# Refilling PSUM with partial sums in the opening of a two-layer decoder trunk, with eight visits instead of five

## The chip, the cores and the metric

The kernel runs on one core of a Trainium2 chip. A core has a matrix engine (TensorE, PE in the profile; its weight loads stand apart as PEld), a vector engine (VectorE, DVE), a scalar engine (ScalarE, ACT), GpSimd (POOL), and SyncE (SP), whose queue issues most transfers. TensorE accumulates in PSUM, which has eight banks of 128 x 512 float32; everything else lives in SBUF or in HBM. The metric is the device time of one execution in microseconds (us); lower is better.

## The reference

512 tokens of width 2048 go through two layers. All of it is float32.

```python
# layer 0: differential attention, 8 heads, q and k of 2 x 128, v and g of 256 a head
c_act = silu(c)
shift, scale, gate = split(c_act @ w_mod[0] + b_mod[0], 3)
h = x * (1 + scale) + shift
q, k, v, g = split(h @ a_w_in, 4)          # a_w_in: 2048 x 8192
a = softmax(q1 k1' + alibi) - lam * softmax(q2 k2' + alibi)
y = (rms_norm(a v) * (1 - lam_init) * silu(g)) @ a_w_out
x = layer_norm(alpha * x + gate * y)
# then shared keys, values and forget gates from x with its own modulation,
# and layer 1: forgetting attention with 16 heads, projections b_w_in and b_w_out
```

The part that matters here is the beginning. `h` needs `shift` and `scale`, which are products of the 2048 activated conditioning values with two 2048 x 2048 blocks of `w_mod`. `h @ a_w_in` for the first two heads can begin as soon as 128 columns of `h` (one k-tile of sixteen) are known.

## The kernel before

**Products.** Every float32 matrix is split into a high part in the matrix engine's format (`hi`, a cast on ScalarE) and the remainder (`lo`, a subtraction on VectorE). A product is three matmuls: hi x hi, hi x lo, lo x hi (`products`, lines 174 to 176).

**Weights.** `WeightStream` holds one fixed order of pieces of two k-tiles by up to 512 columns. SyncE loads a piece into one of four staging tiles (`wst`, line 47); `step` splits it into one of three pairs `whi` (line 94) and `wlo` (line 95). A pair is free again when its last product is done.

**The opening** (the block around `START`) computes `h` k-tile by k-tile and at once the first projections of heads 0 and 1. For one set of k-tiles (first k-tile 0, then 1, then pairs: `sets`) SyncE loads the modulation rows into `sms` (line 473, five buffers), VectorE multiplies them with the conditioning values and adds them up (`sacc`, lines 498 and 500; half of k-tile 1's sum is done by TensorE, line 527), TensorE adds the 128 partial rows (line 530), and VectorE adds the bias (`mcol`, line 536). Then TensorE transposes 128 columns of `x` (line 541), ScalarE writes the high part `hh` and a full copy `htmp` (lines 545 and 546), and VectorE the low part `hl` (line 550).

For each k-tile and head there are seven sums of 128 x 512: three for q and the first half of k (banks 4, 5, 6, named `sc`, `sc` and `o`) and four for v and g (banks 0 to 3, `acc`). That is 21 matmuls for a k-tile and a head. The seven sums of one head fill seven of the eight banks, and the eighth is used for sums and transposes, so only one head can be in PSUM at a time. The kernel therefore works in visits (`phases`): head 0 takes k-tiles 0 to 3, head 1 takes 0 to 7, head 0 takes 4 to 11, head 1 takes 8 to 15, head 0 takes 12 to 15. At the end of a visit `spill` brings the seven sums to SBUF: ScalarE copies them where they are the head's first (line 578), and VectorE adds them to what is there where they are not (line 580).

**Order.** VectorE's order in the opening is the order of the program, which the string `START` spells: a digit is that many multiply-adds of modulation rows, `c` finishes a set and starts its column sums, `m` adds the bias, `t` turns a k-tile, `l` writes its low part, `s` splits the next weight piece, `g` does the products of the next k-tile of a visit. The order of the other engines' instructions is fixed by a planner when the kernel is built: it takes, among instructions that are ready by its own estimate, the one earliest in the program. Each engine then runs its own list strictly in that order; SyncE's transfers too.

After the opening, heads 0 and 1 use the sums in `part`, and the third and later heads are projected in groups that keep all sixteen k-tiles in PSUM.

Of the kernel before, what the change touches and what calls it, by code (L numbers as in the profile page):

```python
# [11 lines left out]
F32R = mybir.dt.float32r  # L12
I32 = mybir.dt.int32
AF = mybir.ActivationFunctionType
ALU = mybir.AluOpType

P = 128
# [10 lines left out]
ET = mybir.EngineType  # L28


START = "cmtlssg6c6t1lgcst4g3tsl9sggts8sl6s2gtggts7lgsstlgg2s7gstl2ss9gsgtslgg5stgg6lsstg2gss8sggt2g4l4sgstctslggtslssggssgggg"
LAM_INIT = 0.8 - 0.6 * math.exp(-0.0)


# [76 lines left out]
def tile_yoco(  # L111
# [24 lines left out]
    V, S, PE, G = nc.vector, nc.scalar, nc.tensor, nc.gpsimd  # L136
# [7 lines left out]
    hpool = ctx.enter_context(tc.tile_pool(name="hpool", bufs=32))  # L144
# [20 lines left out]
    def o_bank(name="o"):  # L165
        return ps.tile([P, 512], F32, name=name, tag="o", bufs=1)
# [2 lines left out]
        S.copy(hi, src)  # L169
        V.tensor_tensor(lo, src, hi.bitcast(F32), op=ALU.subtract)  # L170

    def products(dst, lhs, rhs, start, stop):

        PE.matmul(dst, lhs[0], rhs[0], start=start, stop=False)  # L174
        PE.matmul(dst, lhs[0], rhs[1], start=False, stop=False)  # L175
        PE.matmul(dst, lhs[1], rhs[0], start=False, stop=stop)  # L176


    ident = const.tile([P, P], F32, name="ident")
# [79 lines left out]
    ws = WeightStream(nc, wpool)  # L259
# [38 lines left out]
    Hh = [None] * KT  # L298
    Hl = [None] * KT
# [5 lines left out]
    def group(job, natural, evac, banks=range(4), bg=0, before_sub=None, after_sub=None, hold=0, after_held=None):  # L305
# [7 lines left out]
        def burst(s, b, hi, lo):  # L313
            nonlocal count
            for kk in range(2):
                kt = 2 * s + kk
                bs = slice(b * P, (b + 1) * P)
                start, stop = kt == 0, kt == KT - 1
                if natural:
                    products(acc[b][:, :w], (Hh[kt][:, bs], Hl[kt][:, bs]), (hi[kk][:, :w], lo[kk][:, :w]), start, stop)  # L320
                else:
                    products(acc[b], (hi[kk][:, bs], lo[kk][:, bs]), (Hh[kt], Hl[kt]), start, stop)
            if s == ns - 1:
                evac(b, acc[b])
            tick(bg(count) if callable(bg) else bg)
            count += 1
# [113 lines left out]
    part = {}  # L440
    with tc.tile_pool(name="start", bufs=2, reuse_waits="tile") as sp, tc.manual_schedule(engines={ET.DVE}):
# [18 lines left out]
        loaded = {}  # L460
# [91 lines left out]
        acc = {}  # L552
        wsub = {}

        def first_products(u, kt, start, stop):
            s, kq = kt // 2, kt % 2
            if start:
                acc[u] = [acc_bank() for _ in range(4)] + [sc_bank(), sc_bank(), o_bank()]
            for m, job in enumerate(first[u]):
                if kq == 0:  # L560
                    wsub[u, m] = ws.get(job, s, 0)
                hi, lo = wsub[u, m]
                for b in range(3 if m == 0 else 4):
                    bs = slice(b * P, (b + 1) * P)
                    if m == 0:
                        products(acc[u][4 + b], (hi[kq][:, bs], lo[kq][:, bs]), (Hh[kt], Hl[kt]), start, stop)
                    else:
                        products(acc[u][b], (Hh[kt][:, bs], Hl[kt][:, bs]), (hi[kq], lo[kq]), start, stop)

        def spill(u):  # L570
            new = u not in part
            if new:
                part[u] = [None] * 7
            last = at["go"] == len(todo) - 1
            for b in (0, 1, 4, 6, 5, 2, 3) if last else (4, 5, 6, 0, 1, 2, 3):
                if new:
                    part[u][b] = kpool.tile([P, T], F32, name="part", tag="K")
                    S.copy(part[u][b], acc[u][b])
                else:
                    V.tensor_tensor(part[u][b], part[u][b], acc[u][b], op=ALU.add)  # L580

        todo = [(u, kt, kt == k0, kt == k1 - 1) for u, k0, k1 in phases for kt in range(k0, k1)]

# [59 lines left out]
        while at["go"] < len(todo):  # L643
            go()
            dv(4)
            split_next()
# [539 lines left out]
    acc = [acc_bank() for _ in range(TB)]  # L1186
    held = {}
    for i, (half, s) in enumerate(lag):
# [294 lines left out]
```

## Time and profile before

| | us |
|---|---|
| median of three runs | 1960.49 (1959.22 to 1961.36) |
| the profiled execution | 1958.95 |
| its span, first to last instruction | 1957.2 |
| TensorE busy | 1923.4 |
| VectorE busy | 1355.0 |
| ScalarE busy | 700.0 |
| start of the first product | 18.09 |
| start of the last product of the opening | 200.21 |

A profile is one execution. A row of instructions in order of time gives its start, its duration, the engine, the line, the operation with output and inputs, how many were merged, and in brackets how long the engine had been idle and what ended that. Rows of windows give the busy time of each engine in a stretch, the granted clock of TensorE (1.00 is full) and what the transfers did. A matmul's duration (0.39 us) is longer than the distance to the next one, because they overlap.

### The profile page before, as it was taken

The page shows a single profiled execution, that of the slowest core. Times are in us where ns is not written, and L with a number is a line of the kernel's source. Part 1 is how long each engine was busy: PE and PEld are TensorE (multiplying, and loading weights), DVE is VectorE, ACT ScalarE, POOL GpSimd, SP SyncE. Part 2 cuts the span into 40 slices and gives each one's busy share as a digit, 9 for nine tenths or more (in the row PEclk, how much of TensorE's full clock was granted, in tenths as well). Part 3 has the DMA queues.
Part 4 walks back from the last instruction along what each step waited for, and adds up shares of the span by engine and source line. Part 5 has one row for each costly group of instructions (what it writes and reads, how often), then busy time and mean ns, then how long its engine had stood idle before and what let it go on. Part 6 is the DMA issues. An engine that isn't in the chain of part 4 may idle for free.

```text
span 1957.2 us, 25652 instructions
## 1 busy us (share of the span) xinstructions
PE 1923.4 (98%) x8997; PEld 1619.0 (83%) x8997; DVE 1355.0 (69%) x2499; ACT 700.0 (36%) x1186; POOL 2.2 (0%) x10
## 2 busy tenths in 40 slices
PE   5999999999999999999999999999999999999997
PEld 4888888888888888888889998888888888888886
DVE  7886578767777778567675657776566666676657
ACT  2432444323332344531273223224343434353123
POOL 0000000000000000000000000000000000000000
PEclk8999999999999999999999999999999999999999
DMA  9983355676667675466537866775354555553622
GB/s 343 361 302 118 124 183 166 202 229 204 213 203 224 190 238 177 130 229 214 181 133 233 270 202 215 245 260 163 110 157 148 153 154 153 156 173 113 223 91 104
DMA packets 337582, 376.16 MB, mean 192 GB/s; under 512 B 67974, under 2 KB 247196, under 8 KB 336684
## 3 DMA queue, kind: packets, MB, share of 16 engines
q1 hardware_dynamic: 334496, 370.30, 58.8%
q10 hardware_dynamic: 2956, 4.22, 0.6%
q8 instruction: 71, 1.16, 0.2%
q14 instruction: 59, 0.48, 0.1%
HBM read 345.63 MB, written 28.79 MB: 191 GB/s over the span
## 4 chain that ended last, share of the span: by engine, by line
PE 93%; DVE 3%; DMA 1%; SPq 1%; issue 1%; ACT 0%; DVEq 0%; ACTq 0%
PE acc L174 28%; PE acc L175 28%; PE acc L176 28%; PE sc L174 2%; PE sc L175 2%; PE sc L176 2%; PE o L174 1%; PE o L175 1%; PE o L176 1%; DVE wlo L95 1%; SPq L473 0%; PE tr L541 0%; DMA nr<-n_dram 0%; DMA wst<-in_a_w_in_dram 0%; DVE sacc L500 0%
## 5 line engine op out<-in xcount | busy, mean ns | idle before, releaser
L94 ACT CAST whi<-wst 128x1024 fp32r<-128x1024 f32 (+3 forms) x330 | 333.5, 1011 | 736.5 <-PE acc L176 339.5
L95 DVE TENSOR_TENSOR wlo<-wst,whi 128x1024 fp32r<-128x1024 f32 (+3 forms) x330 | 385.7, 1171 | 280.6 <-ACT whi L94 267.9
L174 PE MATMUL acc<-whi,hh 128*128 128x512 f32 (+1 forms) x1296 | 494.0, 384 | 1.0 <-DVE ztmp L1007 1.0
L175 PE MATMUL acc<-wlo,hh 128*128 128x512 f32 (+1 forms) x1296 | 492.4, 380 | 0.3 <-DVE wlo L95 0.3
L176 PE MATMUL acc<-whi,hl 128*128 128x512 f32 (+1 forms) x1296 | 491.8, 380 | 0.0
L174 PE MATMUL acc<-hh,whi 128*128 128x512 f32 x1184 | 463.6, 392 | 0.0
L175 PE MATMUL acc<-hl,whi 128*128 128x512 f32 x1184 | 461.7, 390 | 0.0
L176 PE MATMUL acc<-hh,wlo 128*128 128x512 f32 x1184 | 460.9, 390 | 0.0
L174 PEld LDWEIGHTS acc<-whi,hh 128*128 128x128 f32 x1296 | 244.5, 189 | 41.0 <-DVE ztmp L1007 1.8
L176 PEld LDWEIGHTS acc<-whi,hl 128*128 128x128 f32 x1296 | 243.2, 188 | 41.7
L175 PEld LDWEIGHTS acc<-wlo,hh 128*128 128x128 f32 x1296 | 243.4, 188 | 38.9 <-DVE wlo L95 0.7
L393 DVE SCALAR_TENSOR_TENSOR macc<-ms,cact,macc 128x512 f32<-128x512 f32 x307 | 229.2, 747 | 56.3 <-DMA ms<-in_w_mod_dram 38.4
L176 PEld LDWEIGHTS acc<-hh,wlo 128*128 128x128 f32 x1184 | 222.3, 188 | 47.7
L174 PEld LDWEIGHTS acc<-hh,whi 128*128 128x128 f32 x1184 | 222.5, 188 | 43.2 <-issue 0.3
L175 PEld LDWEIGHTS acc<-hl,whi 128*128 128x128 f32 x1184 | 222.5, 188 | 42.2
L500 DVE SCALAR_TENSOR_TENSOR sacc<-sms,cact,sacc 128x512 f32<-128x512 f32 (+1 forms) x127 | 89.5, 705 | 5.7 <-DMA sms<-in_w_mod_dram 2.0
L728 ACT ACTIVATE e<-e,mn 128x128 f32<-128x128 f32 (+3 forms) x64 | 36.0, 563 | 103.0 <-DVE mn L724 102.9
L1289 ACT ACTIVATE eb<-eb,mnb 128x128 f32<-128x128 f32 (+1 forms) x64 | 36.0, 563 | 88.8 <-DVE mnb L1286 88.6
L724 DVE CUSTOM_DVE_ANT_0 e<-sc,bias 128x128 f32<-128x128 f32 (+3 forms) x64 | 31.1, 486 | 25.2 <-PE sc L176 25.2
L1286 DVE CUSTOM_DVE_ANT_0 eb<-sc,biasb 128x128 f32<-128x128 f32 (+1 forms) x64 | 31.1, 486 | 23.0 <-PE sc L176 22.4
L393 DVE SCALAR_TENSOR_TENSOR macc<-msk,cact,macc 128x512 f32<-128x512 f32 x53 | 39.7, 749 | 1.0
L1280 DVE SCALAR_TENSOR_TENSOR biasb<-nfb,F,mask 128x128 f32<-128x128 f32 (+1 forms) x64 | 34.6, 542 | 0.6
(264 smaller groups left out, 1714.9 us busy)
## 6 DMA issues: line engine op xcount, KB each, us to landing
wst<-in_a_w_in_dram SPq DMA_DIRECT2D x240, 256.0 KB, 3.8
ms<-in_w_mod_dram SPq DMA_DIRECT2D x136, 256.0 KB, 3.8
ms<-in_kv_w_mod_dram SPq DMA_DIRECT2D x64, 512.0 KB, 4.4
wst<-in_b_w_in_dram SPq DMA_DIRECT2D x128, 256.0 KB, 2.8
sms<-in_w_mod_dram SPq DMA_DIRECT2D x56, 512.0 KB, 6.8
wst<-in_kv_w_dram SPq DMA_DIRECT2D x40, 512.0 KB, 3.8
ms<-in_w_mod_dram SPq DMA_DIRECT2D x32, 512.0 KB, 4.2
wst<-in_a_w_out_dram SPq DMA_DIRECT2D x32, 512.0 KB, 4.2
```

The lines of the kernel that those rows point to most:

```text
L94: self.nc.scalar.copy(hi[:, :, :w], st[:, :, :w])
L95: self.nc.vector.tensor_tensor(lo[:, :, :w], st[:, :, :w], hi[:, :, :w].bitcast(F32), op=ALU.subtract)
L174: PE.matmul(dst, lhs[0], rhs[0], start=start, stop=False)
L175: PE.matmul(dst, lhs[0], rhs[1], start=False, stop=False)
L176: PE.matmul(dst, lhs[1], rhs[0], start=False, stop=stop)
L393: ins = V.scalar_tensor_tensor(acc, w, cact[:, kt : kt + 1], acc, op0=ALU.mult, op1=ALU.add)
L500: V.scalar_tensor_tensor(acc, w, sc, acc, op0=ALU.mult, op1=ALU.add)
L724: V.tensor_tensor_reduce(out=e[:, :w], in0=sc[:, :w], in1=st["bias"][:, (3 - i) * P :], scale=-1.0, scalar=3.0e38, op0=ALU.add, op1=ALU.mi ...
L728: S.activation(e[:, :w], e[:, :w], AF.Exp, bias=mn, scale=-1.0, accum_out=rs)
L1280: V.scalar_tensor_tensor(bias[:, :w], cur[hd, "nf"][:, :w], F[:, i, hd : hd + 1], mask[:, (3 - i) * P :], op0=ALU.add, op1=ALU.add)
L1286: V.tensor_tensor_reduce(out=e[:, :w], in0=sc[:, :w], in1=bias[:, :w], scale=-1.0, scalar=3.0e38, op0=ALU.add, op1=ALU.min, accum_out=mn)
L1289: S.activation(e[:, :w], e[:, :w], AF.Exp, bias=mn, scale=-1.0, accum_out=rs)
```

## The change

Three things change, all in the opening.

1. There are eight visits: head 0 takes k-tile 0, head 1 takes 0 and 1, head 0 takes 1 to 3, head 1 takes 2 to 5, head 0 takes 4 to 7, head 1 takes 6 to 11, head 0 takes 8 to 15, head 1 takes 12 to 15. The order of weight pieces follows the visits; a piece of two k-tiles is listed once, where it is first used.
2. A head that comes back gets its seven partial sums copied into the PSUM banks by ScalarE before its products, which then add to them (`start` is False). At the end of every visit ScalarE copies the sums out; VectorE adds nothing.
3. `START` is written anew for these visits. The first two weight pieces, which head 0 needs in two visits, are split into tiles of the pool of k-tiles, half a piece at a time, and so do not hold one of the three pairs.

```diff
-START = "cmtlssg6c6t1lgcst4g3tsl9sggts8sl6s2gtggts7lgsstlgg2s7gstl2ss9gsgtslgg5stgg6lsstg2gss8sggt2g4l4sgstctslggtslssggssgggg"
+START = "c1msstlgc8mtssg1lggcsmt2lt2lsgg4s4sgg4csmt2lt2lsgg4s4sgg4csmt2lt2lsgg4s4sgg4csmt2lt2lsgg4s44cmt2lt2lsgg4s4sggs4sggcsmt2lt2lsgg444csmtltlsggssggssgg"
...
-    def products(dst, lhs, rhs, start, stop):
+    def products(dst, lhs, rhs, start, stop, loaded=False):
...
-    phases = [(0, 0, 4), (1, 0, 8), (0, 4, 12), (1, 8, 16), (0, 12, 16)]
+    phases = [(0, 0, 1), (1, 0, 2), (0, 1, 4), (1, 2, 6), (0, 4, 8), (1, 6, 12), (0, 8, 16), (1, 12, 16)]
...
-    for u, k0, k1 in phases:
-        for s in range(k0 // 2, k1 // 2):
-            for j in first[u]:
-                ws.add(j, s)
+    for u, s in dict.fromkeys((u, k // 2) for u, k0, k1 in phases for k in range(k0, k1)):
+        for j in first[u]:
+            ws.add(j, s)
...
             if start:
                 acc[u] = [acc_bank() for _ in range(4)] + [sc_bank(), sc_bank(), o_bank()]
+                for b in (4, 5, 6, 0, 1, 2, 3) if u in part else ():
+                    S.copy(acc[u][b], part[u][b])
+            loaded = u in part
+            start = start and not loaded
...
                 if new:
                     part[u][b] = kpool.tile([P, T], F32, name="part", tag="K")
-                    S.copy(part[u][b], acc[u][b])
-                else:
-                    V.tensor_tensor(part[u][b], part[u][b], acc[u][b], op=ALU.add)
+                S.copy(part[u][b], acc[u][b])
...
-                ws.step()
+                ws.step((lambda: hpool.tile([P, 512], F32R, name="held", tag="H")) if ws.done < 2 else None)
                 ws.load(ws.done + 3)
```

More of the change, by code (lines that the diff above doesn't have):

```diff
@@ L170, in split @@
         V.tensor_tensor(lo, src, hi.bitcast(F32), op=ALU.subtract)
-    def products(dst, lhs, rhs, start, stop):
-        PE.matmul(dst, lhs[0], rhs[0], start=start, stop=False)
-        PE.matmul(dst, lhs[0], rhs[1], start=False, stop=False)
-        PE.matmul(dst, lhs[1], rhs[0], start=False, stop=stop)
+    def products(dst, lhs, rhs, start, stop, loaded=False):
+        PE.matmul(dst, lhs[0], rhs[0], start=start, stop=False, skip_group_check=loaded)
+        PE.matmul(dst, lhs[0], rhs[1], start=False, stop=False, skip_group_check=loaded)
+        PE.matmul(dst, lhs[1], rhs[0], start=False, stop=stop, skip_group_check=loaded)
     ident = const.tile([P, P], F32, name="ident")
@@ L565, in first_products @@
                     if m == 0:
-                        products(acc[u][4 + b], (hi[kq][:, bs], lo[kq][:, bs]), (Hh[kt], Hl[kt]), start, stop)
+                        products(acc[u][4 + b], (hi[kq][:, bs], lo[kq][:, bs]), (Hh[kt], Hl[kt]), start, stop, loaded)
                     else:
-                        products(acc[u][b], (Hh[kt][:, bs], Hl[kt][:, bs]), (hi[kq], lo[kq]), start, stop)
+                        products(acc[u][b], (Hh[kt][:, bs], Hl[kt][:, bs]), (hi[kq], lo[kq]), start, stop, loaded)
         def spill(u):
```

## The prediction

> **What bounds the kernel now.** I read the page's engine line and slices first, then windows over the opening, then the groups by form, last the instructions in order of time around one change of visit.
>
> The page of the kernel before (busy shares; busy tenths and granted TensorE clock in forty slices of 49 us; shares of the chain):
>
> ```profile
> PE 1923.4 (98%) x8997; PEld 1619.0 (83%) x8997; DVE 1355.0 (69%) x2499; ACT 700.0 (36%) x1186; POOL 2.2 (0%) x10
> PE   5999999999999999999999999999999999999997
> PEclk8999999999999999999999999999999999999999
> PE 93%; DVE 3%; DMA 1%; SPq 1%; issue 1%; ACT 0%; DVEq 0%; ACTq 0%
> ```
>
> TensorE is the bound, and only the first and last slices are not full. Windows: length, then busy time and instructions of PE, weight load, VectorE (DVE), ScalarE (ACT) and POOL, granted clock, DMA share, GB/s:
>
> ```profile
> 0.00:18.05 18.05, 2.64 (x10) 1.99 (x10) 8.99 (x24) 4.17 (x6) 1.61 (x9) 1.00 0.91 279
> ...
> 33.00:37.00 4.00, 3.99 (x9) 3.14 (x10) 3.23 (x5) 0.63 (x1) 0.00 (x0) 0.50 1.09 385
> ...
> 40.60:43.40 2.80, 1.68 (x12) 1.39 (x12) 2.73 (x6) 1.03 (x3) 0.00 (x0) 1.00 1.07 380
> 43.40:47.00 3.60, 3.52 (x11) 2.79 (x12) 2.43 (x4) 0.70 (x2) 0.00 (x0) 0.57 1.09 381
> 47.00:59.00 12.00, 12.00 (x54) 9.98 (x53) 11.68 (x16) 6.11 (x11) 0.00 (x0) 0.99 1.09 383
> 59.00:200.00 141.00, 141.00 (x668) 116.93 (x668) 103.70 (x146) 47.07 (x65) 0.56 (x1) 1.00 0.72 243
> 200.00:400.00 200.00, 199.83 (x952) 167.36 (x950) 146.54 (x347) 85.52 (x176) 0.00 (x0) 1.00 0.56 170
> 400.00:1957.00 1557.00, 1543.18 (x7215) 1302.73 (x7213) 1060.43 (x1933) 550.96 (x924) 0.00 (x0) 1.00 0.57 184
> ```
>
> From 59 to 200 us TensorE has no gap; VectorE is busy 104 of 141 us, so its additions there cost nothing now. After 200 nothing waits until the tail: a microsecond won or lost in the opening arrives unchanged at the end. Before 18.05 nothing changes, since the first k-tile needs the same transfers. What is left is 18.05 to 59.
>
> How much TensorE loses there: the products of L174, L175 and L176, the sums L527, then the column sums L530 and transposes L541 at full rate, and the first and last of the 21 products of one k-tile for one head:
>
> ```profile
> 18.05:59.00 40.95, 14.51 (x37) 0.87 1.09 382
> 18.05:59.00 40.95, 13.72 (x32) 0.87 1.09 382
> 18.05:59.00 40.95, 12.99 (x32) 0.87 1.09 382
> 18.05:59.00 40.95, 3.77 (x32) 0.87 1.09 382
> 59.00:200.00 141.00, 5.67 (x48) 1.00 0.72 243
> 59.00:200.00 141.00, 7.18 (x48) 1.00 0.72 243
> 195.68 0.39 PE L174 MATMUL sc<-hh,whi 128*128 128x512 f32 x1
> 200.21 0.39 PE L176 MATMUL acc<-whi,hl 128*128 128x512 f32 x1
> ```
>
> A product takes (200.21 - 195.68)/20 = 0.2265 us. In 18.05 to 59 stand 37 + 32 + 32 = 101 products, 22.9 us; the 32 sums, 3.8; twelve column sums at 5.67/48 = 0.118, 1.4; twelve transposes at 7.18/48 = 0.150, 1.8. Together 29.9 of 40.95 us: **11.0 us are lost**, in gaps and at half clock. No change of the opening can win more than that.
>
> **The change, part by part.** Durations by form (count, then busy us and mean ns; idle before):
>
> ```profile
> L94 ACT CAST whi<-wst 128x1024 fp32r<-128x1024 f32 x16 | 16.9, 1057 | 32.0 <-PE o L175 17.8 <-issue 12.2 <-ACT htmp L546 0.9
> L94 ACT CAST whi<-wst 128x512 fp32r<-128x512 f32 x2 | 1.2, 624 | 7.8 <-PE o L175 5.9 <-PE acc L176 1.8
> L545 ACT ACTIVATE hh<-tr,mcol 128x512 fp32r<-128x512 f32 x16 | 12.5, 778 | 38.9 <-PE tr L541 38.9
> L578 ACT COPY part<-acc 128x512 f32<-128x512 f32 x8 | 4.4, 613 | 0.3
> L580 DVE TENSOR_TENSOR part<-part,acc 128x512 f32<-128x512 f32 x10 | 6.3, 680 | 0.0
> L500 DVE SCALAR_TENSOR_TENSOR sacc<-sms,cact,sacc 128x512 f32<-128x512 f32 x105 | 78.9, 751 | 4.1 <-DMA sms<-in_w_mod_dram 1.2
> L95 DVE TENSOR_TENSOR wlo<-wst,whi 128x1024 fp32r<-128x1024 f32 x16 | 19.5, 1221 | 10.0 <-ACT whi L94 10.0
> L95 DVE TENSOR_TENSOR wlo<-wst,whi 128x768 fp32r<-128x768 f32 x16 | 15.2, 952 | 0.0
> ```
>
> And the visit that ends at 55 us: ScalarE's spill copies up to its next cast, and TensorE's last product into the first bank and first product of the next visit:
>
> ```profile
> 52.90 1.08 ACT L578 COPY part<-sc 128x512 f32<-128x512 f32 x2 [4.05 <-PE sc L176]
> 53.86 0.61 ACT L578 COPY part<-o 128x512 f32<-128x512 f32 x1
> 54.34 2.09 ACT L578 COPY part<-acc 128x512 f32<-128x512 f32 x4
> 56.25 1.12 ACT L94 CAST whi<-wst 128x1024 fp32r<-128x1024 f32 x1
> ```
> ```profile
> 52.47 0.39 PE L176 MATMUL sc<-hh,wlo 128*128 128x512 f32 x1
> ...
> 55.19 0.39 PE L174 MATMUL sc<-hh,whi 128*128 128x512 f32 x1
> ```
>
> *Removed:* three times seven additions on VectorE, 21 x 0.68 = 14.3 us. They lie under TensorE's full 141 us, so they win nothing by themselves.
>
> *Added on ScalarE:* five visits become eight. Spills go from 14 copies to 56, and six visits start by copying seven sums back, 42 more: 84 added. Seven spills take 56.25 - 52.90 = 3.35 us, 0.48 each. No copy into PSUM stands in the trace; the nearest rows are this 0.48 and the 0.62 of a 128x512 cast from SBUF; I take 0.5 and keep 0.48 to 0.62. That is 84 x 0.5 = 42 us more, on a ScalarE that is busy 47 of 141 us: room enough over the stage, but bunched at the changes of visit. The Trainium skill (ScalarE: Activation LUTs, Step-by-step: what each stage is for) says ScalarE writes faster to PSUM than to SBUF; by that the price is at or under 0.48, the 42 us become 40 or less, and no run here shows it yet.
>
> *A change of visit.* A bank must be finished, spilled, refilled and only then multiplied into. The old visit's last k-tile ends its banks three products (0.68 us) apart, so TensorE still has 6 x 0.68 = 4.1 us of work when the first bank is done, and uses the last bank of the new visit another 4.1 us later. ScalarE needs 14 x 0.5 = 7 us in these 8.2. If spills and refills take turns, bank n is ready 1.0(n+1) us after the first was done and is needed at 4.1 + 0.68 n: no wait (7.0 against 8.2 for the last). But a cast of 1.06 us and activations of 0.78 us for the next k-tiles want the same 8 us. Five of the six refilling visits find two k-tiles ready, so TensorE can take a ready bank twice; the visit to k-tile 1 alone cannot. Lower end 0 each; upper end as in the first rival, 2.0. I take 0.4 for five of them and 0.8 for that one: **2.8 us**.
>
> *The order of visits.* Head 1 now takes k-tiles 0 and 1 before head 0 goes on. The transfers ahead of head 1's first weights are those that stood ahead of head 0's second: the kernel before issues them at the same place in SyncE's queue and shows when they land. Rows of SyncE, ScalarE and TensorE:
>
> ```profile
> 23.54 5.01 SPq L47 DMA_DIRECT2D wst<-in_a_w_in_dram  x6
> ...
> 31.45 0.83 ACT L94 CAST whi<-wst 128x768 fp32r<-128x768 f32 x1 [12.74 <-DMA wst<-in_a_w_in_dram]
> 32.18 0.77 ACT L545 ACTIVATE hh<-tr,mcol 128x512 fp32r<-128x512 f32 x1
> ...
> 33.01 1.22 PE L174 MATMUL sc<-hh,whi 128*128 128x512 f32 x2 [1.58 <-ACT hh L545]
> ```
>
> So head 1 can start when that cast ends, at 32.3, as its k-tile 0 is long there; if k-tile 1's two activations go first, 2 x 0.7 later at 33.6. I take 32.3. From 18.05 to 32.3 TensorE does 21 products (4.8 us), the sums of k-tile 1 (3.8 + 4 x 0.118) and four transposes (0.6): 9.7 of 14.25, lost **4.6 us**. Then it is cold, as now: between 33 and 37 nine products in 4.00 us at clock 0.50 instead of 17.7, lost **2.0 us**. After that it has 63 products (14.3 us) for k-tiles 0 and 1 instead of 21, so the gap of 40.6 to 43.4 and the second cold stretch after it (clock 0.57) are covered: this is where the change can win. I estimate k-tile 2 at 48 us (VectorE does two more splits, 1.22 + 0.95, and ScalarE one train of 14 copies before it) against a need at 51; each us beyond the cover would cost one.
>
> *Later supply.* Two heads on a pair of k-tiles are 84 products, 19 us. VectorE needs for a pair 16 x 0.75 + 4 splits (2 x 1.22 + 2 x 0.95) + 2 x 0.69 = 17.7 us, so the chain stays ahead, except at k-tiles 8 to 11, which head 1 takes alone. There VectorE must do, after a split buffer comes free inside k-tile 7: a cast 1.06, a split 1.22, twelve multiply-adds 9.0 and a split 0.95, 12.2 us; then column sums 0.95, transposes 0.6, an activation 0.78, some 2.5 with the column add. TensorE has 12 products of k-tile 7 (2.7) and two k-tiles (9.5), with their transposes 13 to 14. Between 0.6 and 2.8 us open up at k-tile 10; I take **1.6 us**.
>
> *The rest.* SyncE's weight loads come earlier than modulation rows; bytes are the same, and at 383 GB/s (47 to 59 us) they bound only what is counted above. The first two splits go to eight tiles of the k-tile pool, in halves, 2.2 us on VectorE as before. Products, their count and shape stay; a product onto a refilled bank is the same instruction.
>
> *Sum.* Lost after: 4.6 + 2.0 + 1.6 + 2.8 = 11.0 us, against 11.0 now: **no change**. The profiled execution took 1958.95 us (span 1957.2), 1.5 under the median of 1960.49; I put the difference of 0.0 on the median: 1960.5 us. Least loss: without waits and gap, 6.6, that is -4.4 us. Within 0.2% means 3.9 us, about what a measurement of this kernel can tell from no change.
>
> **Rivals.**
> *Copies on the path (slower).* ScalarE's order is fixed when the kernel is built. If all seven spills stand ahead of the refills, the last spill ends 4.1 + 0.5 us after the first bank was done and the first refill at 5.1, while TensorE is free at 4.1: 1.0 us each; with a 1.06 us cast between, 2.0. Six times: 6 to 12 us instead of 2.8, +3.2 to +9.2, middle 1966.7. For it: seven copies stand unbroken at 52.90 to 56.25. Against: there was nothing to put between. It decides from 1.1 us a change on. Chance 0.28.
>
> *Short waits cool the clock (slower).* If each refilling visit starts cold, as at 33 and 43.4, six cost 2.0 more: +12, 1972.5. For it: the window of 2.80 us with 1.68 busy at 40.6 was followed by 3.6 us at 0.57. Against: waits here should be under 2 us amid dense products. The Trainium skill (TensorE: Matmul & The Clock Gate, A second HAM failure mode: psum-queue depth-cycling) describes just such micro-idling between banks that lowers the clock; but the same page (What's actually happening) lets the clock fall only after an idle window of about 3.4 us, by which waits of 2 us would cost themselves alone. Chance 0.08.
>
> *Everything is hidden (faster).* Spills and refills alternate and k-tile 10 is in time: -4.4, 1956.1; without the cold start at 32.3 another 2.0, 1954.1. For it: the sums above leave 1.2 us of room at a change. Against: five mean waits of zero. Chance 0.22.
>
> **How the numbers follow.** My forecast has 0.42, its own range -3.9 to +3.9 (a late first cast, +1.3, and the k-tile 10 bounds included): 0.36 within 0.2%, 0.02 faster, 0.04 slower. Copies on the path: 0.26 slower, 0.02 within. Clock: 0.08 slower. Hidden: 0.20 faster, 0.02 within. Faster 0.22, same 0.40, slower 0.38. The range runs from 1954.5 (nearly all of the hidden case) to 1970 (all copies on the path), leaving out the clock case and little more.
>
> **What would show it.** TensorE's first product for head 1 at 32.3 to 33.6 and no gap at 40; products dense from there; L580 gone and 84 more copies on ScalarE; idle of TensorE released by ScalarE's refill line, 0 to 1 us at each of six changes; a gap of 1 to 3 us before k-tile 10; the last product of the opening within 4 us of 200.2; nothing moved after it. I am wrong if waits on refills exceed 1.1 us each, if the clock falls after them, or if weights or k-tiles 2 and 3 come later than their cover.

## The result: 22 us slower

The changed kernel takes 1982.65 us (median of four runs, 1982.29 to 1985.63) against 1960.86 us for the kernel before beside it (1959.22 to 1961.36): a ratio of 1.0115, 95% interval 1.0102 to 1.0127. The forecast was 1960.5 us, no change; its range ended at 1970. The two profiled executions lie 26.7 us apart (1985.63 and 1958.95), 5 us more than the medians, so what the traces below count is somewhat more than the 21.8 us of the medians.

The profiled execution took 1985.63 us, the longest of the four, with a span of 1983.8. The lines of its page that answer to those of before (engines, slices of 49.6 us, granted clock, chain):

```profile
PE 1934.9 (98%) x8997; PEld 1625.3 (82%) x8997; DVE 1342.9 (68%) x2480; ACT 742.7 (37%) x1272; POOL 2.2 (0%) x10
...
PE   5988999999999999999999999999999999999997
...
PEclk9989999999999999999999999999999999999999
...
PE 92%; DVE 4%; DMA 2%; ACT 1%; issue 1%; SPq 1%; DVEq 0%; ACTq 0%
```

Two more slices are not full. Windows over the same profile (columns as in the prediction: length, busy time and instructions of PE, PEld, DVE, ACT and POOL, clock, DMA share, GB/s), and the last product of the opening:

```profile
0.00:19.25 19.25, 2.63 (x10) 1.99 (x10) 11.47 (x29) 4.35 (x8) 1.60 (x9) 1.00 0.90 275
19.25:59.00 39.75, 34.78 (x156) 28.84 (x157) 25.08 (x39) 19.98 (x34) 0.00 (x0) 0.87 0.98 329
59.00:227.00 168.00, 154.53 (x670) 124.56 (x669) 106.72 (x149) 85.54 (x143) 0.56 (x1) 0.93 0.66 218
227.00:427.00 200.00, 199.83 (x951) 167.11 (x950) 139.30 (x333) 81.94 (x166) 0.00 (x0) 1.00 0.57 170
427.00:1983.00 1556.00, 1543.13 (x7215) 1302.85 (x7214) 1060.32 (x1934) 550.91 (x924) 0.00 (x0) 1.00 0.59 185
```
```profile
226.84 0.39 PE L176 MATMUL acc<-whi,hl 128*128 128x512 f32 x1
```

The opening ends at 226.84 instead of 200.21, 26.6 us later. Behind it the two kernels are alike: 199.83 busy of 200 us, then the same 7215 TensorE instructions in 1556 and 1557 us. Where 668 TensorE instructions had filled 141 us without a gap, 670 now take 168 us with 13.5 us idle, at a mean clock of 0.93.

Counted in the traces, start in us of the n-th of the 672 products of the opening (`after` is the changed kernel; the other columns are experiments below):

| product | before | after | e4 | e11 | e17 | e18 | e19 |
|---|---|---|---|---|---|---|---|
| 84 | 55.0 | 50.4 | 50.5 | 51.0 | 45.7 | 55.2 | 46.6 |
| 126 | 65.9 | 64.9 | 60.9 | 61.4 | 57.4 | 66.2 | 56.2 |
| 168 | 76.0 | 74.6 | 72.1 | 72.6 | 67.2 | 76.1 | 69.0 |
| 252 | 96.9 | 98.8 | 93.5 | 94.1 | 89.9 | 97.1 | 91.3 |
| 336 | 117.9 | 123.1 | 116.6 | 116.1 | 114.1 | 118.0 | 113.7 |
| 420 | 138.8 | 156.7 | 143.4 | 143.7 | 147.8 | 139.2 | 137.7 |
| 504 | 159.3 | 175.8 | 163.9 | 164.8 | 167.0 | 159.7 | 158.8 |
| 588 | 180.7 | 207.7 | 193.9 | 186.0 | 198.9 | 181.5 | 179.8 |
| 672 | 200.2 | 226.8 | 213.1 | 205.2 | 218.1 | 201.0 | 199.4 |

The early gain is there: 4.6 us at product 84. Most of it is gone by product 126 and all of it by product 252; then 13 us are lost between products 336 and 420 and 10 between 504 and 588.

The first loss is at k-tile 2, whose first product is the 85th:

```profile
50.38 0.39 PE L176 MATMUL acc<-held,hl 128*128 128x512 f32 x1
...
50.60 0.95 PE L529 MATMUL tr<-ones,sacc 128*128 128x1 f32 x8
51.59 0.16 DVE L535 TENSOR_TENSOR mcol<-tr,bcol 128x4 f32<-128x4 f32 x1 [5.84 <-PE tr L529]
...
53.33 0.73 PE L174 MATMUL sc<-hh,whi 128*128 128x512 f32 x2 [0.87 <-ACT hh L544]
```

VectorE has stood still for 5.84 us when the column sums of k-tiles 2 and 3 come, behind product 84; only then can k-tile 2 be finished.

**Where it goes.** The queries of what VectorE waited for (us in total, times, longest) from 18.05 us to the end of the opening, before and then after:

```profile
DVE wlo L95 <- ACT whi L94: 17.2, 6, 5.9
DVE hl L550 <- ACT htmp L546: 13.1, 5, 3.5
DVE mcol L536 <- PE tr L530: 8.6, 6, 2.8
```
```profile
DVE mcol L535 <- PE tr L529: 28.8, 7, 8.5
DVE wlo L95 <- ACT whi L94: 23.7, 10, 5.9
DVE hl L549 <- ACT htmp L545: 14.0, 13, 2.7
```

The bias now waits 28.8 us for the column sums, 8.6 before. And TensorE's own waits from 19 to 227 us after:

```profile
PE sc L174 <- ACT hh L544: 6.9, 8, 0.9
PE tr L529 <- DVE sacc L499: 6.7, 2, 3.8
PE tr L540 <- DVE mcol L535: 5.4, 8, 3.6
```

No matmul there waits for the copies back into PSUM (line 560; by the groups, weight loads wait for them 1.8 us in all). TensorE waits for VectorE's last multiply-add, the bias and the activation: the chain that makes a k-tile. Rows in order of time, after, around k-tiles 8 to 11 (start, duration; in brackets the idle time before and what ended it):

```profile
123.06 0.39 PE L176 MATMUL acc<-whi,hl 128*128 128x512 f32 x1
...
123.28 0.95 PE L529 MATMUL tr<-ones,sacc 128*128 128x1 f32 x8
124.27 0.16 DVE L535 TENSOR_TENSOR mcol<-tr,bcol 128x4 f32<-128x4 f32 x1 [5.05 <-PE tr L529]
...
124.49 0.66 PE L540 MATMUL tr<-ident,xt 128*128 128x128 f32 x4 [0.26 <-DVE mcol L535]
125.18 0.78 ACT L544 ACTIVATE hh<-tr,mcol 128x512 fp32r<-128x512 f32 x1 [3.59 <-PE tr L540]
...
126.01 0.72 PE L174 MATMUL sc<-hh,whi 128*128 128x512 f32 x2 [0.87 <-ACT hh L544]
...
135.97 0.39 PE L176 MATMUL acc<-whi,hl 128*128 128x512 f32 x1
...
140.19 1.83 PE L529 MATMUL tr<-ones,sacc 128*128 128x1 f32 x8 [3.83 <-DVE sacc L499]
```

Until 123.06 TensorE does products without a gap, and VectorE has nothing to do for 5.05 us: its next instruction is the bias, which needs the column sums, and these stand in TensorE's list behind those products. When they are done at last, TensorE has no product left, and sums, bias, transposes and activation run one after the other with nothing beside them. Then VectorE has to do the next pair's multiply-adds, which it could have done in the 5.05 us; it isn't done when TensorE needs the sums, and TensorE stands still for 3.83 us. The two engines wait for each other in turns. Two windows of after, from one bias to the next:

```profile
75.83:100.03 24.20, 23.07 (x100) 18.60 (x100) 16.87 (x24) 13.76 (x22) 0.00 (x0) 0.93 0.93 315
100.03:124.27 24.24, 23.11 (x100) 18.68 (x100) 16.87 (x24) 13.77 (x22) 0.00 (x0) 0.93 0.78 260
```

VectorE works 16.87 us for a pair of k-tiles, and the pair takes 24.2.

**The clock.** Windows of after, ahead of and in two stretches at half clock:

```profile
98.50:101.90 3.40, 2.27 (x17) 1.84 (x16) 1.57 (x3) 0.96 (x2) 0.00 (x0) 1.00 0.70 237
101.90:105.30 3.40, 3.40 (x11) 2.71 (x12) 2.11 (x3) 1.57 (x3) 0.00 (x0) 0.50 0.10 13
136.00:139.40 3.40, 0.36 (x2) 0.00 (x0) 3.22 (x6) 0.83 (x1) 0.00 (x0) 1.00 1.08 373
139.40:149.60 10.20, 8.29 (x27) 6.71 (x28) 6.47 (x11) 2.89 (x4) 0.00 (x0) 0.50 0.75 256
```

In the opening the trace has half clock from 30.2 (6.8 us), 54.1, 78.0 and 101.9 (3.4 each), 139.4 (10.2) and 194.1 (6.8): 34 us, against 10.2 before. From product 84 to the end of the opening, intervals between TensorE's instructions add up to some 20 us of gaps and some 11 us of products and transposes slowed at half clock (each interval beyond the one at full clock, counted to at most twice that); before it was 2 to 3 and none.

### The profile page after: what moved, and what is told of

Read it like the earlier page. It is cut to its first block, busy times and chain, and to the rows that moved or that the text cites. A ratio compares the mean times of both kernels' runs of the same rounds, so it can differ in the third digit from the quotient of the medians.

```text
span 1983.8 us, 25712 instructions
## 1 busy us (share of the span) xinstructions
PE 1934.9 (98%) x8997; PEld 1625.3 (82%) x8997; DVE 1342.9 (68%) x2480; ACT 742.7 (37%) x1272; POOL 2.2 (0%) x10
## 4 chain that ended last, share of the span: by engine, by line
PE 92%; DVE 4%; DMA 2%; ACT 1%; issue 1%; SPq 1%; DVEq 0%; ACTq 0%
PE acc L174 27%; PE acc L175 27%; PE acc L176 27%; PE sc L174 2%; PE sc L175 2%; PE sc L176 2%; PE o L174 1%; DVE sacc L499 1%; PE o L175 1%; PE o L176 1%; DVE wlo L95 1%; DMA sms<-in_w_mod_dram 1%; PE tr L540 1%; DMA wst<-in_a_w_in_dram 1%; SPq L472 0%
```

## The experiments

Three accounts are set against each other. Theory A (also D, order theory or list theory): the order of VectorE's and TensorE's lists. Theory B (also refill theory): the copies back into PSUM. Theory C is in e1 to e8 that eight visits leave TensorE no products in reserve, whatever the order; in the later runs it is the transfers, or the three pairs of split weights. Edits of `START` are shown for one pair of k-tiles as it recurs; all times are medians against a kernel before of 1959.6 to 1960.3 us on the same chip. Groups of runs had different chips, so that differences between groups carry about 1 us.

**e1: sums earlier.** The column sums (`c`) stand ahead of the products of the last two k-tiles (`gg`); VectorE's list is unchanged.

```diff
-csmt2lt2lsgg4s4sgg4
+cggsmt2lt2lsgg4s4s4
```

> The changed kernel with the letters of START moved so that the column sums of a set stand in the program ahead of the last two products of the visit before; VectorE's own order stays the same instruction for instruction, as do visits, copies and products. Theory A (order of sums): the changed kernel is slow because TensorE's list has the column sums behind all products of a visit, so that VectorE waits 3.4 to 8.5 us at each bias addition and the chain of sums, bias, transposes and activation lies open at each set; then this kernel wins back most of the 26 us of the opening, 1960 to 1969 us, and VectorE's waits on the column sums fall under 2 us each. Theory B (refills): the 84 copies on ScalarE are the cost; then it stays at 1978 to 1984. Theory C (visits): eight visits leave TensorE no products in reserve, whatever the order; then it stays over 1975 too, with gaps before new k-tiles.

1979.81 us (ratio 1.0101, 1.0086 to 1.0116): only 3 us better, far from theory A's range. The wait moved on by one step, as VectorE's row for the low part shows, in the query as above, 14.0 us in the changed kernel:

```profile
DVE hl L549 <- ACT htmp L545: 36.3, 10, 9.3
```

**e4: the whole turn earlier.** Sums, bias, transposes and low parts ahead of the products that were in front of them; VectorE's list unchanged.

```diff
-csmt2lt2lsgg4s4sgg4
+csmt2lt2lggsgg4s4s4
```

> As the kernel with the sums first, but the bias, both transposes of the next two k-tiles and their low parts stand ahead of those products in the program too; VectorE's order is again the same. Theory A: the transposes now overlap with products as well, so that TensorE has no stretch of low activity between visits and no second to sixth half-clock stretch; 1957 to 1964 us, 2 to 6 us under the kernel with only the sums moved. Theory B: 1978 to 1984. Theory C: gaps at new k-tiles stay, over 1975.

1973.05 us (1.0067, 1.0052 to 1.0082): 9.6 us of the loss are TensorE's order alone, and the time lies between the ranges of the theories. Until product 336 this kernel is ahead of the kernel before; what remains is lost behind it.

**e6: only VectorE's list.** Multiply-adds of the next pair are put in front of VectorE's waits for bias and low parts.

```diff
-csmt2lt2lsgg4s4sgg4
+c5smt4lt4lsgg2s1sgg
```

> The changed kernel with its visits, copies and TensorE's order of sums behind the products; only VectorE's list is written otherwise: of the sixteen multiply-adds of the next set, five stand between a set's last sum and its bias, four before each low part, and three after (changed kernel: none, two and twelve). Theory D (VectorE waits in its own order): the late k-tiles come from VectorE standing still at bias and low part, 42.8 us up to the last k-tile against 21.7 in the kernel before; with work in front of each wait the last k-tile comes at 175 to 188 us instead of 199 and the time is 1960 to 1972. Theory C (visits without reserve): TensorE has no products left at each new set whatever VectorE does; the last k-tile stays past 193 and the time over 1975.

1980.16 us (1.0107, 1.0091 to 1.0123): 2.5 us, hardly clear of the scatter (1978.76 to 1986.09 here, 1982.29 to 1985.63 for the change). By its expectation this was the outcome of theory C. But VectorE's bias still waits 24.0 us for the sums (to 200 us): its own list alone does not take that wait away.

**e7: both.**

```diff
-csmt2lt2lsgg4s4sgg4
+c5smt4lt4lggsgg2s1s
```

> VectorE's waits filled as in the kernel with the waits filled, sums, bias and transposes ahead of the last products of the visit before in the program, and the bias of k-tile 0 ahead of the second multiply-add of k-tile 1. Theory D: VectorE no longer waits over 35 us in all, TensorE has its sums early; 1956 to 1964, at best 4 us faster than the kernel before (the 4.6 us won up to the 84th product, less refills). Theory C: gaps before k-tiles 10 and 14 stay, 1968 to 1980.

1967.09 us (1.0036, 1.0023 to 1.0049): 15.6 us back, between the two ranges. This is not the two edits alone, for its `START` also begins in another way (shown with e9): its first product is late (23.4 us), as TensorE's share of k-tile 1's sums, which waits for transfers, came ahead of the first products. With the beginning of the changed kernel (e9) the same two edits give back 12.2 us, as much as e4's 9.6 and e6's 2.5 together. Neither list is the whole cause.

**e2: additions instead of copies back.** Eight visits and the changed `START`, but VectorE adds the partial sums as before.

```diff
-                for b in (4, 5, 6, 0, 1, 2, 3) if u in part else ():
-                    S.copy(acc[u][b], part[u][b])
-            loaded = u in part
-            start = start and not loaded
+            loaded = False
...
-                S.copy(part[u][b], acc[u][b])
+                    S.copy(part[u][b], acc[u][b])
+                else:
+                    V.tensor_tensor(part[u][b], part[u][b], acc[u][b], op=ALU.add)
```

> The eight visits and the new START, but without the copies into PSUM: a returning head starts new sums and VectorE adds them to the old ones at the end of its visit, as in the kernel before; 42 additions on VectorE (25 to 29 us) in place of 42 refills and 42 spill copies. Theory A: the sums still stand behind the products and VectorE has more to do; 1982 or more, up to 2005. Theory B: the loss is gone, 1960 to 1968. Theory C: 1978 to 2000.

1998.91 us (1.0200, 1.0183 to 1.0217): 16 us worse than the change. The 42 copies back, with 42 more copies out, are therefore the better way in these visits. Additions that had cost nothing under TensorE's full 141 us cost here, where VectorE is late, at some 0.69 us each. From the groups of e2 (busy, mean ns, idle before), the largest of the three kinds:

```profile
L581 DVE TENSOR_TENSOR part<-part,acc 128x512 f32<-128x512 f32 x22 | 14.7, 686 | 0.0
```

**e3: copies back in the kernel before.** Its five visits and its `START`, three of them refilled, no additions.

```diff
+                for b in (4, 5, 6, 0, 1, 2, 3) if u in part else ():
+                    S.copy(acc[u][b], part[u][b])
+            loaded = u in part
+            start = start and not loaded
...
-                    S.copy(part[u][b], acc[u][b])
-                else:
-                    V.tensor_tensor(part[u][b], part[u][b], acc[u][b], op=ALU.add)
+                S.copy(part[u][b], acc[u][b])
```

> The kernel before, with its five visits, its weight order and its START, but with the partial sums copied back into PSUM by ScalarE and no additions: 21 refills and 21 spills more on ScalarE, 21 additions fewer on VectorE. Theory A: three refilling visits cost 0 to 1 us each, 1959 to 1965. Theory B: half of the changed kernel's refills, half of its loss, 1970 to 1976. Theory C: no loss, 1959 to 1963.

1962.46 us (1.0013, 1.0004 to 1.0022), 2.9 us slower.

**e14b and e14: no copies back.** The changed kernel, and e11 below, with the refill left out.

```diff
-                for b in (4, 5, 6, 0, 1, 2, 3) if u in part else ():
-                    S.copy(acc[u][b], part[u][b])
-            loaded = u in part
+            loaded = False
```

> The changed kernel with the 42 copies back into PSUM left out: each visit of a head starts its sums anew and the partial sums of the visits before are lost (that part of the computation is missing). Order theory (VectorE's and TensorE's lists carry the loss): only the price seen in e3_before_refill goes, 0.6 to 0.9 us for each of six visits, 3.6 to 5.4 us, so 1977 to 1979. Refill theory (the copies stand ahead of activations and casts in ScalarE's list and so delay the lists of the others): more than 10 us go, under 1973.

> e11_late_fill with the 42 copies back into PSUM left out (the partial sums of earlier visits are missing from the result). If the 5 us that e11 still loses are the refills: 1959.5 to 1961.3. If they are the remaining waits at the changes of set: 1963 to 1965.

1983.53 us (1.0117, 1.0102 to 1.0132) beside 1982.65 with them, and 1964.42 (1.0021, 1.0012 to 1.0030) beside e11's 1964.85. In these two kernels the copies back cost nothing that can be measured; theory B falls, and my 0.6 to 0.9 us a visit, taken from e3, with it. Of the 2.9 us of e3, 0.7 are matmuls that wait for a copy back; what cost the rest is open.

**e8: the regular order on the kernel before.** Its five visits and additions, `START` in one regular pattern for each pair.

```diff
-... ts8sl6s2gtggts7lgsstlgg2s7gstl2ss9g ...
+... cssmt2lt2lgg4ss4gg4cssmt2lt2lgg4ss4gg4 ...
```

> The kernel before, with its five visits and VectorE's additions, but VectorE's order spelled in the regular manner of the change: nothing between a set's last sum, its bias, and two multiply-adds before each low part. Theory D: VectorE waits over 40 us up to the last k-tile and the time is 1970 to 1985. Theory C: the visits keep two k-tiles of products in reserve at each new set, so sums and transposes find their place and the waits do not reach TensorE; 1958 to 1965.

1966.76 us (1.0034, 1.0022 to 1.0047): an order of this kind costs 7 us without any other part of the change. Neither expectation is met, and the wait is not the one of the changed kernel: up to 181 us VectorE waits 22.1 us at the low parts (13.1 in the kernel before) and 0.4 at the biases.

**e9 and e10: the start, and the pairs.** e9 is e7 with the start of the changed kernel; e10 is e9 with the first eight weight pieces, not two, split into tiles of the k-tile pool.

```diff
-cmt1sslgc8mtssg1l
+c1msstlgc8mtssg1l
```
```diff
-                ws.step((lambda: hpool.tile([P, 512], F32R, name="held", tag="H")) if ws.done < 2 else None)
+                ws.step((lambda: hpool.tile([P, 512], F32R, name="held", tag="H")) if ws.done < 8 else None)
```

> Sums, bias and transposes ahead of the products and multiply-adds in front of VectorE's waits, as in e7_fill_turn_first, but with the start of the changed kernel (bias of k-tile 0 behind the multiply-add of k-tile 1). Theory A (the waits of VectorE on column sums and transposes are the loss, and e7 lost some 4 us only because its first product stood at 23.4 us): the first product is back at 19.3 us and the time 3 to 4 us below e7's 1967.1, so 1963 to 1964. Theory C (the transfers and the three pairs of split weights set the pace after the start, whatever the order): the early gain is given back by product 252 and the time is that of e7, 1966 to 1968.

> As e9_both_orders, with the first eight weight pieces split into tiles of the k-tile pool instead of the first two, so that VectorE's splits do not wait for one of the three pairs there. Theory C (the pairs are the limit): VectorE's wait on ScalarE's cast of the next piece falls from 27 us in e7 to under 12 us, and the time falls 3 to 6 us below e9. Theory A (only the order counts): within 1.5 us of e9.

1970.49 us (1.0054, 1.0039 to 1.0069) and 1966.99 (1.0040, 1.0025 to 1.0055). e9 misses both expectations: the first product is at 19.3 us, but product 84 at 52.3, later than e7's 50.1, with 10.2 us at half clock from 29.6. Of e10 no verdict: 3.5 us better than e9, as theory C had it, but see e11.

**e11: e4's early part, filled waits from k-tiles 8 and 9 on.**

```diff
-csmt2lt2lggs4s44cmt2lt2lggsgg4s4sggs4scsmt2lt2lggs444
+c4smt4lt4lggs4sc4mt4lt4lggsgg4ssggssc4smt4lt4lggs4
```

(against e4), and the same with eight pieces in the k-tile pool (e11_held8).

> e4_turn_first up to the fourth set of k-tiles, which was 1.3 us ahead of the kernel before at product 336 of the opening, and from there on multiply-adds in front of VectorE's waits as in e6. Theory A: the gaps of e4 after product 336 (33 us until product 420 and from 504 to 588) close to 21 to 24 us, and the time falls to 1958 to 1963. Theory C: the lead is lost again after product 336 and the time stays above 1966.

> As e11_late_fill with the first eight weight pieces in tiles of the k-tile pool. Theory A: within 1.5 us of e11_late_fill. Theory C: 3 to 6 us less, and if it is under 1958.5 the refilled visits beat the kernel before.

e11: 1964.85 us (1.0026, 1.0016 to 1.0035), 17.8 us back by `START` alone, to a time between the ranges of A and C. With eight pieces in the pool 1967.02 (1.0038, 1.0023 to 1.0053): 2 us worse where it was 3.5 better for e9, so the three pairs are not the limit of e11. Window and VectorE's waits of e11 (window of waits 18.05 to 199 us):

```profile
59.00:205.50 146.50, 142.01 (x656) 113.44 (x655) 104.33 (x147) 81.40 (x137) 0.56 (x1) 1.00 0.73 246
```
```profile
DVE wlo L95 <- ACT whi L94: 24.1, 11, 5.1
DVE hl L549 <- ACT htmp L545: 15.4, 8, 3.6
```

The wait of the bias, 28.8 us in the changed kernel, is down to 0.9, and behind 59 us no stretch at half clock is left. From product 504 to 588 it needs 21.2 us as the kernel before does (21.4); 336 to 420 still takes 27.6.

**e16a and e16b: can the early gain be kept?** The fourth visit (head 1, k-tiles 2 to 7) and all later ones are long as before; only the two early returning visits are refilled; from product 126 on VectorE's order is that of the kernel before. The two differ in the join.

```diff
-    phases = [(0, 0, 1), (1, 0, 2), (0, 1, 4), (1, 2, 6), (0, 4, 8), (1, 6, 12), (0, 8, 16), (1, 12, 16)]
+    phases = [(0, 0, 1), (1, 0, 2), (0, 1, 4), (1, 2, 8), (0, 4, 12), (1, 8, 16), (0, 12, 16)]
...
+        REFILL = ((0, 1), (1, 2))
```

> A mixed version, nothing left out: head 0 takes k-tile 0, head 1 takes 0 and 1, head 0 takes 1 to 3, head 1 takes 2 to 7, and then the long visits of the kernel before; only the two early visits that come back are refilled, the later ones use VectorE's additions as before; from product 126 on VectorE's order is that of the kernel before, ahead of it that of e11_late_fill, joined by a bias, a turn and eight multiply-adds. If order and refills are the whole account: the 4.4 us won by product 84 less two refills of 0.6 to 0.9, so 2.6 to 3.2 us under the kernel before, 1956.5 to 1957.3. If the early gain can't be kept because VectorE is not ahead at product 126: 1960 to 1966.

> As e16a, with the join exactly in the order of the kernel before (turn, eight multiply-adds, low part, eight multiply-adds). Same expectations: 1956.5 to 1957.3 if order and refills are the whole account, 1960 to 1966 if VectorE is not ahead at product 126; the two differ by under 2 us if the join does not matter.

1967.86 us (1.0043, 1.0026 to 1.0060) and 1969.49 (1.0046, 1.0031 to 1.0061): slower still than the range I gave. e16a is 4.9 us ahead of the kernel before at product 126 (61.0 against 65.9) and 4.3 at 168, then takes 32.1 us for the next 84 products where the kernel before takes 20.9. The low part of k-tile 4, in e16a and then in the kernel before:

```profile
77.85 0.68 DVE L549 TENSOR_TENSOR hl<-htmp,hh 128x512 fp32r<-128x512 f32 x1
```
```profile
68.32 0.69 DVE L550 TENSOR_TENSOR hl<-htmp,hh 128x512 fp32r<-128x512 f32 x1
```

TensorE came earlier, the k-tile later; what makes it later there was not told apart.

**e17, e18 and e19: half of the modulation rows not loaded**: the changed kernel, the kernel before, e11.

```diff
-                t = sp.tile([P, nr, 2, nk * P], F32, name="sms", tag="sms", bufs=NBUF)
+                if k // nr % 2:
+                    t = loaded[i, k - nr]
+                else:
+                    t = sp.tile([P, nr, 2, nk * P], F32, name="sms", tag="sms", bufs=NBUF)
...
```

The loads behind it move under the `else` as well.

> The changed kernel with half of the modulation rows of the opening not loaded: every second tile of rows stands for the one before it, so VectorE's and TensorE's work, order and waits in their lists are the same and half of those transfers are gone (the modulation of the result is wrong in this way). List theory (an instruction at the head of an engine's own list waits for another engine): the difference to e18_before_half_rows stays at 15 to 25 us. Transfer theory (stalled transfers are what comes late): it falls under 8 us.

> The kernel before with the same half of the rows not loaded. Both theories: faster than the kernel before by an earlier first product, 2 to 8 us; the pace after product 84 as before, within 3 us until product 672, as TensorE has no gap there. Were the transfers a bound of it there, nothing could be seen.

> e11_late_fill with the same half of the rows not loaded. Transfer theory (what e11 still loses is transfers that stood still between 45 and 60 us and again at 90 to 105): within 2 us of e18_before_half_rows or under it. List theory: 4 to 6 us above it, as e11_late_fill is above the kernel before.

1977.16 us (1.0091, 1.0074 to 1.0107), 1958.97 (0.9993, 0.9984 to 1.0003) and 1959.69 (1.0000, 0.9991 to 1.0010). For e18 a time 2 to 8 us shorter was expected; its 1.3 us are not clear of the interval, and its first product is only 0.2 us earlier. Between e17 and e18 there are still 18.2 us: the change loses that with half of the rows out of the way, and the bias of e17 waits nearly as it did (to 180 us; 28.4 us with all rows):

```profile
DVE mcol L538 <- PE tr L532: 25.5, 6, 8.5
```

Between e19 and e18 there is 0.7 us, so e11's loss goes with the transfers. But most of it is won at the start: of the 5.8 us by which e19's last product is ahead of e11's, 4.4 are there at product 84. From product 84 to 672 e11 needs 154.2 us, e19 152.8, the kernel before 145.2 and e18 145.8. So even with the lists in order and half of the rows gone, the eight visits lose 7.0 us behind product 84, nearly the 8.6 us that they are ahead there. TensorE's largest wait in that stretch of e19 is for the copies back (line 563 there); the rest of the 7.0 us was not told apart:

```profile
PE sc L174 <- ACT sc L563: 2.9, 3, 1.0
```

That transfers fell behind in the changed kernel is seen in what SyncE's load of rows waited for in the whole opening, before (to 174 us) and then after (to 200 us):

```profile
SPq L473 <- DVE sacc L500: 13.0, 10, 3.0
```
```profile
SPq L472 <- DVE sacc L499: 46.5, 18, 6.8
...
SPq L472 <- DVE sacc L497: 11.4, 4, 3.9
```

A tile of rows is free when its last multiply-add is done. In the changed kernel VectorE stands at the bias, the tiles stay taken, and SyncE's list stands behind the first load that needs one. In e11 these loads still wait 34.4 us (to 170 us) although its biases wait 0.9; what holds its tiles was not told apart. The windows from 18.05 to 110 us show 318 GB/s in the changed kernel, 342 in e11 and 357 before:

```profile
18.05:110.00 91.95, 83.90 (x369) 68.28 (x368) 62.27 (x90) 49.30 (x80) 0.00 (x0) 0.91 0.94 318
```
```profile
18.05:110.00 91.95, 88.70 (x403) 70.42 (x402) 68.84 (x98) 56.44 (x94) 0.00 (x0) 0.98 0.99 342
```
```profile
18.05:110.00 91.95, 87.73 (x405) 72.48 (x406) 74.87 (x106) 33.58 (x47) 0.00 (x0) 0.94 1.02 357
```

**The account.** The change loses 21.8 us. Of these 17.8 go with the two lists put in order (the change against e11; some 17 if each is taken against the kernel before on its own chip), and it is 17.5 with half of the rows gone (e17 against e19). The 18.2 of e17 against e18 hold visits and copies as well. The remaining 4 to 5 go when half of the rows are not loaded (e11 to e19: 5.2; the change to e17: 5.5; the kernel before gains 1.3 from it), most of them ahead of product 84; in e17 and e19 the first product is 1.9 and 1.7 us earlier. The copies back take no measurable part in the changed kernel and in e11; the 42 copies out that were added were not taken away by themselves. That eight visits stay over 1975 us whatever the order is refuted by e11, but behind product 84 they were never as fast as five. No version that was run beats the kernel before.

## Why the prediction was wrong

**The step that failed** is *Later supply*: "VectorE needs for a pair … 17.7 us, so the chain stays ahead, except at k-tiles 8 to 11". The 17.7 us are right as work: the windows show 16.87. They are not the time of a pair, which is 24.2 us, where 84 products take 20.9 in the kernel before. I took the busy time of an engine for its period. An in-order list needs its work plus its waits, and the order that makes these waits stands in `START`: `sgg4s4sgg4csm` has the products of two k-tiles (`gg`) ahead of `c`, and only one split between `c` and the bias `m`. Those are 42 products or 9.5 us, and VectorE stood at seven biases for 28.8 us, 8.5 at the longest. In the kernel before the same wait is 8.6 us in all, and its trace had it. I named both lists and costed the order of neither. The estimate of k-tile 2 "at 48 us … against a need at 51" failed by the same step: the need was right (product 84 at 50.38), but its first product stands at 53.33, as VectorE's 5.84 us in front of the bias were put at nothing.

*The gap at k-tile 10*, taken as 1.6 us (0.6 to 2.8), was in the right place. The 84 products that hold it take 33.6 us instead of 20.9, 12.7 more: above all 3.83 us of gap, then sums, transposes and the first products in 10.2 us at half clock. The upper bound assumed VectorE at work all the time and TensorE at full clock. The bounds do not come out of their own terms either: 12.2 and 2.5 us less 13 to 14 give 0.7 to 1.7, and less 12.2, without the transposes, 2.5.

*Early gain.* Right in size: head 1 takes over after one k-tile (at 34.60 us, 1.0 later than the later of the two times I gave), the gap of 40.6 to 43.4 is gone, one stretch of half clock ahead of 50 us is left, and product 84 comes 4.6 us earlier. The sum had 4.4 there (11.0 less 4.6 and 2.0). That it is so close is in part luck, as the first product and head 1 came later than the sum has them. That it would last to the end was the error: TensorE was 4.6 us ahead of a chain that was itself later. The low part of k-tile 2 starts at 53.98 (46.0 in the kernel before) and that of k-tile 4 at 78.2, 3.6 us behind product 168, where before it starts at 68.32, 7.7 us ahead of it.

*"Before 18.05 nothing changes."* Wrong by 1.2 us: the first product stands at 19.29, since the new `START` puts a multiply-add of k-tile 1, which waits for its transfer, ahead of k-tile 0's bias.

*Refilling visits*, 2.8 us in the sum: zero by e14 and e14b, and no matmul of the changed kernel waits on line 560. Such waits stand in the openings of e3 (0.7 us in all) and e19 (2.9) alone. The price of a copy was 0.5 us, with 0.62 as the upper end. The groups of after, by form:

```profile
L582 ACT COPY part<-acc 128x512 f32<-128x512 f32 x32 | 17.6, 610 | 0.0
...
L560 ACT COPY acc<-part 128x512 f32<-128x512 f32 x24 | 13.3, 634 | 0.0
...
L582 ACT COPY part<-sc 128x512 f32<-128x512 f32 x16 | 9.3, 587 | 28.3 <-PE sc L176 28.2
...
L560 ACT COPY sc<-part 128x512 f32<-128x512 f32 x12 | 7.2, 602 | 0.3
```

In a row they follow at 0.52 us, the copies out at 0.48. The Trainium skill (ScalarE: Activation LUTs, Step-by-step: what each stage is for) has ScalarE write faster to PSUM than to SBUF; here 602 and 634 ns into PSUM stand against 587 and 610 out of it, so no gain is seen (the sources differ, so this is no clean test of the destination).

*Removed additions*: nothing won under TensorE's full time, as said of the kernel before. But e2 shows that in the new visits they would have cost 16 us. The same 0.68 us instruction is free or not by whether VectorE's list is ahead.

*The rest.* "Bytes are the same" was true and not enough: with half of the rows gone the change gains 5.5 us. I looked at what SyncE issues earlier, not at what its list would wait for.

*The rivals.* Copies on the path (0.28): wrong, zero. Everything hidden (0.22): its premise on the copies held, that on k-tile 10 and its time did not. Short waits cool the clock (0.08): the nearest, but by another cause. Stretches at half clock came after the exposed sums and transposes, not after waits on banks, and they cost some 11 us beside 20 of gaps; they went when the order was mended (e11: none behind 59 us). The Trainium skill (TensorE: Matmul & The Clock Gate, What's actually happening) lets the clock fall after an idle window of about 3.4 us of a free-running monitor. The lengths agree (3.4, 6.8, 10.2), and so do the starts (54.1, 78.0 and 101.9 are 23.9 apart, seven times 3.41). "Idle" does not: in 98.50 to 101.90 TensorE was busy 2.27 of 3.40 us, and half clock followed; yet 2.28 of 3.40 us in 177.00 to 180.40 were followed by full clock. The rival that was missing is the plain one: VectorE's and TensorE's lists waiting for each other in turns.

## What to carry to other kernels

Work per period is a bound only for an engine that never waits: where two in-order lists feed each other, write down for each wait what stands ahead of the awaited instruction in the other list, and add that to the period. A lead of the bound engine in an early stage was worth nothing here, where the engine that feeds it gained no lead too. When the order of two lists is changed, judge both together: here one alone gave 2.5 or 9.6 us, both 12.2 to 17.8.

## What the runs showed of the hardware

In the changed kernel half clock followed three windows of 3.40 us in which TensorE was at work 2.27 or 2.28 us, in sums, transposes and a few products (from 50.70, 74.60 and 98.50), but not the window from 177.00, also with 2.28: busy time alone does not tell when the clock halves. Half clock ended behind a window full of work: the 10.2 us after the gap of 3.83 us are three windows of 3.41 us, in which TensorE was at work 2.37, 2.55 and 3.41 us, and the 6.8 us from 194.10 are two, with 2.53 and 3.40.

Half of the modulation transfers taken away leave the kernel before where it is (0.9993, 0.9984 to 1.0003), although the DMA share stood at 1.08 to 1.10 in the windows of its opening from 18 to 90 us: there a full transfer queue was no bound.
